# Modulation steps of the first MLP, two at every second place instead of one at each

## The chip, the cores and the metric

The kernel runs on one core of one Trainium2 chip, so there is one span and one granted clock to look at. The metric is the device time of one execution in microseconds (us): the median of several executions of the same program. A profile of one more execution gives the trace; times in it count from the start of its span.

## What is computed

A two-layer backbone for 128 context and 512 latent tokens of width 1024 (640 columns in all): layer 0 has attention and a convolution module, layer 1 a recurrent block, and each layer ends in an MLP. Every layer is modulated: six vectors of width 1024 for each of the two condition vectors come from one product with a large weight matrix.

```python
def _adaln(cond, w_mod, b_mod):
    return jnp.split(jax.nn.silu(cond) @ w_mod + b_mod, 6, axis=-1)

def _modulate(x, g, shift, scale):
    return _rmsnorm(x, g) * (1 + scale) + shift

def _sq_relu_mlp(h, w1, w2):
    return jnp.square(jax.nn.relu(h @ w1)) @ w2

# in each layer li, with ms = _adaln(cond_lat, w_mod[li], b_mod[li]) (mp likewise for the context):
y_s = y_s + ms[2] * os_
y_s = y_s + ms[5] * _sq_relu_mlp(_modulate(y_s, norm_ffn[li], ms[3], ms[4]), w_ff1[li], w_ff2[li])
```

## The kernel before

Activations lie transposed: 128 channels on the partitions, 640 token columns as two halves of 320. Products in full precision are made of three matmuls: weights and activations are split into a high part (`whi`, `hh`, `fh`; by a copy on ACT) and a low part (`wlo`, `hl`, `fl`; by a subtraction on DVE), and high x high, high x low and low x high are added up in PSUM (`product`, line 115, and `times`, line 809; every matmul is issued at line 113).

**An MLP** (`mlp`, line 724) goes over four groups `g` of 1024 hidden channels. In the up stage eight units `f` of 128 hidden channels each take 48 matmuls (`up`, line 756) into a PSUM tile `p2`, of which there are two; `hidden` (line 766) then normalizes the unit on DVE (`normed`, line 266: the product `fr`, then the small copy `bs`, after which the PSUM tile is free), applies relu and square on ACT, and at every second unit splits the pair of units into seven combinations for the down stage (`hidden_pair`, line 734). The down stage (`down`, line 806) is a fast 2x2 product: for each of four pairs `j` of output tiles seven blocks of 12 matmuls, some into the pair's `p2` tile, some into an extra bank `bu`. The last two blocks of a pair, `third_` and `fourth`, are put into the list `late` and issued within the next pair. The first unit of group `g+1` is made before the down stage of group `g`, the second one between its last two blocks.

**The modulation product** of the second layer is hidden in the MLP of the first. `mod_gen` (line 308) is a generator; one call of `next` is one **step**: it takes a buffer `mraw` (there are `NM` = 2), issues the transfer of 512 KB of `w_mod` from SyncE's queue (SP, line 313), and issues four matmuls of 32 stationary columns and 256 moving columns (`mod_mm`, line 289, matmul at line 292). The profile has eight records for the four matmuls of one step. Eight steps make one half of a `[128, 512]` PSUM tile, after which DVE transposes it (`mod_finish`, line 295). Three generators of 16 steps, 48 steps in all, stand in the list `fill` when the first MLP begins (line 909), and `filler(n)` (line 321) makes the next `n` steps, or fewer if none are left.

`filler(nfill)` is called at 56 **places** of an MLP: after each of the 32 units (line 772), and 24 times in the down stages, after `third_` and after `fourth` of the pair before (lines 837 and 845). In the first MLP `nfill` is 1, in the second 0. So the 48 steps lie one at each of the first 48 places: 14 places a group, the last one after unit 5 of group 3.

What is issued when on an engine is set by the framework's scheduler from the order of the program; weight transfers and splits have a priority of 4000 instructions ahead (`weights`, line 96, and `block`, line 789). Each engine, SP among them, then works off its own list in order.

Of the kernel before, what the change touches and what calls it, by code (L numbers as in the profile page):

```python
# [36 lines left out]
def backbone(ctx, tc, vecs, xT, wmod, w_att, w_ao, w_ff1, w_ff2, w_li, w_lo, w_lg, kcT, vc,  # L37
# [16 lines left out]
    def P2():  # L54
        if spare and next(turn_) % 3 == 2:
            return spare[0].tile([128, 2, 512], F32, name="p3", tag="p3")
        return ps.tile([128, 2, 512], F32, name="p2", tag="p2", bufs=2)
# [54 lines left out]
    def mm(o, w, v, start=False, stop=False, **kw):  # L112
        nc.tensor.matmul(o, w, v, start=start, stop=stop, **kw)  # L113
# [24 lines left out]
    def add_half(n, h, src, gate):  # L138
        for q, a, b, o, s in PIECE:
            if q == h:  # L140
                v = x[:, n, o:o + b - a]
                nc.vector.scalar_tensor_tensor(v, src[:, a:b], gate[:, n, s:s + 1], v, op0=ALU.mult, op1=ALU.add)  # L142
# [178 lines left out]
    def filler(n):  # L321
        while n and fill:
            try:
                next(fill[0])
                n -= 1
            except StopIteration:
                fill.pop(0)
# [396 lines left out]
    def mlp(l, pre, gate, pool, nfill, nxt, banks):  # L724
# [4 lines left out]
        def relu(r, p):  # L729
            bs = normed(r, p)  # L730
            for q, (a, b) in enumerate(SEG):
                nc.scalar.activation(r[:, a:b], r[:, a:b], AF.Relu, bias=bs[:, q:q + 1])  # L732

        def hidden_pair(r0, r1, all_):

            for r in (r0, r1):
                nc.scalar.activation(r, r, AF.Square)
            n = 8 if all_ else 7
            fh, fl = (pool.tile([128, n, 320], F32R, name=t, tag=t, bufs=4) for t in ("fh", "fl"))
            T = pool.tile([128, 4, 320], F32, name="T", tag="T")  # L740
            b12, b11, b22, b21 = r0[:, 0:320], r0[:, 320:640], r1[:, 0:320], r1[:, 320:640]
            nc.vector.tensor_tensor(T[:, 0], b12, b11, op=ALU.subtract)
            nc.vector.scalar_tensor_tensor(T[:, 1], b22, -1.0, T[:, 0], op0=ALU.mult, op1=ALU.subtract)
            nc.vector.tensor_tensor(T[:, 2], T[:, 1], b21, op=ALU.add)
            nc.vector.scalar_tensor_tensor(T[:, 3], b22, -1.0, b12, op0=ALU.mult, op1=ALU.subtract)
            for s, v in ((slice(0, 1), b11), (slice(1, 3), r1), (slice(3, 5), T[:, 0:2]), (slice(5, 7), T[:, 2:4]),
                         (slice(7, 8), b12))[:n - 3]:
                h, o = (t[:, s].rearrange("p k t -> p (k t)") for t in (fh, fl))
                if len(v.shape) > 2:
                    v = v.rearrange("p k t -> p (k t)")  # L750
                split(h, o, v)
            return fh, fl

        hid, held = {}, {}

        def up(g, f):
            wh, wl = weights(w_ff1[l, g * 8 + f])
# [8 lines left out]
        def hidden(g, f, p):  # L766
            r = held[f % 2] = pool.tile([128, 640], F32, name="fr", tag="t", bufs=4)
            pre.then(lambda: relu(r, p))
            if f % 2:
                r0 = held[0]  # L770
                pre.then(lambda: hid.update({f // 2: hidden_pair(r0, r, l == 1 and g == 3)}))
            filler(nfill)

        def both(g, f):
            hidden(g, f, up(g, f))

        def blocks_of(g, pairs):

            raw, k, t = {}, count(), []

            def ready(v):
                i = next(k) % 2
                if i == 0:
                    t[:] = parts_tile()
                o = slice(i * 512, i * 512 + 512)
                split(t[0][:, o], t[1][:, o], v)
                return t[0][:, o], t[1][:, o]

            def block(j, name):
                with tc.high_priority(offset=4000):  # L790
                    if name == "A11":
                        raw[j] = [raw_unit(w_ff2[l, g * 8 + 2 * j + i]) for i in range(2)]
                    X, Y = raw[j]
                    x0, x1, y0, y1 = X[:, 0:512], X[:, 512:1024], Y[:, 0:512], Y[:, 512:1024]
                    if name == "S1":
                        nc.vector.tensor_tensor(x0, x0, y0, op=ALU.subtract)
                        nc.vector.tensor_tensor(y0, y0, y1, op=ALU.subtract)
                    if name == "S2":
                        nc.vector.scalar_tensor_tensor(y0, x0, -1.0, y1, op0=ALU.mult, op1=ALU.subtract)
                    if name == "S4":  # L800
                        nc.vector.tensor_tensor(x1, x1, y0, op=ALU.add)
                    return ready(dict(A11=x0, A12=x1, A22=y1, S1=y0, S2=y0, S3=x0, S4=x1)[name])

            return block

        def down(g, pairs, between, done):
            block = blocks_of(g, pairs)

            def times(o, j, w, c, ks=range(4), start=True, wb=None):
                wh, wl = wb or block(j, w)  # L810
                for i in ks:
                    fh, fl = hid[i]
                    cs = slice(i * 128, i * 128 + 128)
                    vh, vl = fh[:, COMBO[c]], fl[:, COMBO[c]]
                    mm(o, wh[:, cs], vh, start=start and i == 0, skip_group_check=True)
                    mm(o, wh[:, cs], vl, skip_group_check=True)
                    mm(o, wl[:, cs], vh, stop=i == 3, skip_group_check=True)
                return wh, wl

            late = []  # L820

            def pair(j):
                p, u = P2(), U_[j % 2][:, 0:320]
                a, f = p[:, 0, 0:320], p[:, 1, 0:320]
                n0, n1 = 2 * j, 2 * j + 1
                if j == 0:
                    w1, w5 = times(a, j, "A11", "11", range(3)), times(f, j, "S1", "T1", range(3))
                    times(a, j, "", "11", [3], wb=w1)
                    times(f, j, "", "T1", [3], wb=w5)
                else:  # L830
                    times(a, j, "A11", "11")
                    times(f, j, "S1", "T1")
                nc.scalar.activation(u, a, AF.Copy)  # L833
                add_half(n1, 0, f, gate)
                while late:
                    late.pop(0)()
                    filler(nfill)
                    break
                times(a, j, "A12", "21", start=False)
                add_half(n0, 1, a, gate)  # L840
                times(u, j, "S2", "T2", start=False)
                add_half(n0, 0, u, gate)
                while late:
                    late.pop(0)()
                    filler(nfill)
                times(f, j, "S4", "22", start=False)
                add_half(n0, 0, f, gate)
                done(n0)

                def third_():  # L850
                    times(u, j, "S3", "T3", start=False)
                    add_half(n1, 0, u, gate)

                def fourth():
                    times(u, j, "A22", "T4", start=False)
                    add_half(n1, 1, u, gate)
                    done(n1)

                late.extend((third_, fourth))

            for j in pairs:
                pair(j)
            late.pop(0)()
            between()
            late.pop(0)()
# [3 lines left out]
        for g in range(4):  # L869
# [10 lines left out]
            def between(g=g):  # L880
                if g < 3:
                    begun[g + 1, 1] = up(g + 1, 1)
# [22 lines left out]
    with ExitStack() as ff:  # L905
        pool = ff.enter_context(tc.tile_pool(name="ff0", bufs=1, reuse_waits="tile"))
        banks = ff.enter_context(tc.tile_pool(name="pb0", bufs=1, space=PSUM, reuse_waits="tile"))
        for g in range(3):
            fill.append(mod_gen(1, g, mp))
        nm = mlp(0, nm, MOD[0, 2][:, 8:16], pool, 1,  # L910
                 lambda: Norm(pool, SC[1, 0], MOD[1, 0][:, 0:8]), banks)
# [171 lines left out]
    with ExitStack() as ff:  # L1083
        pool = ff.enter_context(tc.tile_pool(name="ff1", bufs=1, reuse_waits="tile"))
        banks = ff.enter_context(tc.tile_pool(name="pb1", bufs=1, space=PSUM, reuse_waits="tile"))
        mlp(1, nm, MOD[1, 2][:, 8:16], pool, 0, lambda: Final(pool), banks)
# [102 lines left out]
```

## Time and profile before

| | us |
|---|---|
| median of 3 runs | 1448.15 (1445.07 to 1448.96) |
| the profiled execution, its own time | 1448.06 |
| its span in the trace | 1446.3 |
| PE busy | 1403.6 (97% of the span) |
| weight loads (PEld) busy | 1307.6 (90%) |
| DVE busy | 1040.3 (72%) |
| ACT busy | 732.2 (51%) |

The 48 steps of the first MLP lie between 318.8 and 709 us of the span; the second MLP takes its last third. A group of matmul records shows its start, and a busy time that overlaps the next record, since matmuls are pipelined; the pace is read from start to start.

### The profile page before, as it was taken

What the parts mean: (1) busy time and instruction counts of PE and PEld (TensorE: products, weight loads), DVE (VectorE), ACT (ScalarE), POOL (GpSimd) and SP (SyncE); (2) the same over time, 40 slices, a digit from 0 to 9 for tenths busy, and PEclk for the clock granted to TensorE, in tenths of its full rate; (3) what the DMA queues carried; (4) which work ended last, traced back from release to release, by engine and by line L of the source; (5) the groups of instructions that cost most, each with busy time, mean ns of one, the idle gap of its engine ahead of it and who ended that gap; (6) DMA issues with size and microseconds to landing.
All of it is one profiled execution on the core that took longest, in us unless ns stands there. A gap on an engine that the chain in (4) does not pass through costs nothing.

```text
span 1446.3 us, 23687 instructions
## 1 busy us (share of the span) xinstructions
PE 1403.6 (97%) x9567; PEld 1307.6 (90%) x9567; DVE 1040.3 (72%) x1881; ACT 732.2 (51%) x1170; POOL 80.9 (6%) x122
## 2 busy tenths in 40 slices
PE   6999998999999999999999999999999999999998
PEld 4998563999999999999989999999999999999997
DVE  6699784675765675675588699997676676686673
ACT  5333377455434533533555878835643543544553
POOL 0000660000000000000000023100000000000000
PEclk9999899999999999999999999999999999999999
DMA  8523506224253244334212122122213113113112
GB/s 325 195 77 129 175 2 207 84 100 137 85 185 136 94 141 169 109 132 163 71 59 103 59 73 74 59 75 87 74 48 119 67 59 117 59 59 117 44 59 73
DMA packets 42909, 151.87 MB, mean 105 GB/s; under 512 B 4913, under 2 KB 5681, under 8 KB 42801
## 3 DMA queue, kind: packets, MB, share of 16 engines
q1 hardware_dynamic: 42800, 150.38, 29.8%
q8 instruction: 75, 1.23, 0.3%
q14 instruction: 34, 0.27, 0.1%
HBM read 147.60 MB, written 2.76 MB: 104 GB/s over the span
## 4 chain that ended last, share of the span: by engine, by line
PE 84%; DVE 7%; ACT 4%; DMA 2%; issue 1%; POOL 1%; SPq 0%; ACTq 0%; POOLq 0%
PE p L113 66%; PE bu L113 11%; PE p L292 4%; DMA mraw<-in_wmod 2%; DVE wlo L66 1%; PE p L428 1%; PE p L608 1%; DVE xc L968 1%; DVE ib L1027 1%; ACT whi L98 1%; PE p L604 1%; ACT hh L186 1%; DVE t L1019 0%; POOL dg L425 0%; DVE ib L1020 0%
## 5 line engine op out<-in xcount | busy, mean ns | idle before, releaser
L98 ACT ACTIVATE whi<-wraw 128x512 fp32r<-128x512 f32 (+1 forms) x327 | 246.3, 779 | 455.8 <-PE p L113 336.4
L113 PE MATMUL p<-hh,whi 128*128 128x320 f32 (+1 forms) x1512 | 462.6, 313 | 3.1 <-ACT hh L186 1.7
L113 PE MATMUL p<-hl,whi 128*128 128x320 f32 (+1 forms) x1512 | 460.1, 311 | 0.2 <-DVE hl L187 0.2
L113 PE MATMUL p<-hh,wlo 128*128 128x320 f32 (+1 forms) x1512 | 350.4, 310 | 0.0
L66 DVE TENSOR_TENSOR wlo<-wraw,whi 128x512 fp32r<-128x512 f32 (+1 forms) x327 | 280.0, 879 | 46.2 <-ACT whi L98 44.7
L113 PEld LDWEIGHTS p<-hh,whi 128*128 128x128 f32 x1512 | 285.9, 189 | 15.9 <-issue 7.8
L113 PEld LDWEIGHTS p<-hl,whi 128*128 128x128 f32 x1512 | 286.4, 189 | 0.9 <-DVE hl L187 0.8
L113 PEld LDWEIGHTS p<-hh,wlo 128*128 128x128 f32 x1512 | 256.8, 189 | 0.9 <-issue 0.8
L113 PE MATMUL p<-fh,whi 128*128 128x320 f32 x528 | 166.6, 316 | 4.0 <-ACT whi L98 1.1
L113 PE MATMUL p<-fl,whi 128*128 128x320 f32 x528 | 163.5, 310 | 2.0 <-DVE fl L66 2.0
L113 PE MATMUL p<-fh,wlo 128*128 128x320 f32 x528 | 163.3, 310 | 0.9 <-DVE wlo L66 0.9
L142 DVE SCALAR_TENSOR_TENSOR x<-p,mod,x 128x320 f32<-128x320 f32 (+2 forms) x228 | 96.5, 451 | 58.6 <-PE p L113 55.7
L268 DVE TENSOR_TENSOR fr<-p,R 128x640 f32<-128x640 f32 x64 | 52.7, 823 | 101.6 <-PE p L113 101.6
L113 PE MATMUL bu<-fh,whi 128*128 128x320 f32 x360 | 113.2, 314 | 0.3 <-ACT bu L833 0.3
L113 PEld LDWEIGHTS p<-fh,whi 128*128 128x128 f32 x528 | 99.5, 189 | 14.0 <-issue 5.1
L113 PE MATMUL bu<-fl,whi 128*128 128x320 f32 x360 | 112.2, 312 | 0.0
L113 PE MATMUL bu<-fh,wlo 128*128 128x320 f32 x360 | 112.0, 311 | 0.0
L732 ACT ACTIVATE fr<-fr,bs 128x512 f32<-128x512 f32 (+1 forms) x128 | 65.2, 555 | 78.6 <-DVE bs L270 78.4
L113 PEld LDWEIGHTS p<-fl,whi 128*128 128x128 f32 x528 | 99.5, 189 | 2.4 <-DVE fl L66 2.4
L113 PEld LDWEIGHTS p<-fh,wlo 128*128 128x128 f32 x528 | 99.3, 188 | 1.7 <-DVE wlo L66 1.7
L292 PE MATMUL p<-mraw,base 128*32 128x256 f32 x768 | 66.6, 419 | 15.2 <-DMA mraw<-in_wmod 15.0
L409 DVE SCALAR_TENSOR_TENSOR z<-u,vt,z 128x655 f32<-128x655 f32 x90 | 79.6, 911 | 0.4
(225 smaller groups left out, 2043.2 us busy)
## 6 DMA issues: line engine op xcount, KB each, us to landing
wraw<-in_w_ff SPq DMA_DIRECT2D x128, 512.0 KB, 3.5
mraw<-in_wmod SPq DMA_DIRECT2D x96, 512.0 KB, 3.9
wraw<-in_w_li SPq DMA_DIRECT2D x16, 512.0 KB, 3.4
wraw<-in_w_att SPq DMA_DIRECT2D x14, 512.0 KB, 3.6
wraw<-in_w_ao SPq DMA_DIRECT2D x8, 512.0 KB, 3.5
wraw<-in_w_lo SPq DMA_DIRECT2D x8, 512.0 KB, 3.5
x<-in_xT SPq DMA_DIRECT2D x4, 640.0 KB, 8.7
wraw<-in_w_lg SPq DMA_DIRECT2D x4, 512.0 KB, 3.4
```

Source lines behind the costliest of these rows:

```text
L66: nc.vector.tensor_tensor(out, full, f32(hi), op=ALU.subtract)
L98: nc.scalar.activation(hi, raw, AF.Copy)
L113: nc.tensor.matmul(o, w, v, start=start, stop=stop, **kw)
L142: nc.vector.scalar_tensor_tensor(v, src[:, a:b], gate[:, n, s:s + 1], v, op0=ALU.mult, op1=ALU.add)
L186: nc.scalar.activation(h, v, AF.Copy, scale=S[:, kt, s:s + 1])
L268: nc.vector.tensor_tensor(hy(o), p[:, :, 0:320], R, op=ALU.mult)
L292: nc.tensor.matmul(p[32 * q:32 * q + 32, half * 256:half * 256 + 256], base[:, kt], raw[:, q * 256:q * 256 + 256], start=(kt == 0), stop=( ...
L409: nc.vector.scalar_tensor_tensor(z, u[:, k:k + 655], wv[:, k:k + 1], z, op0=ALU.mult, op1=ALU.add)
L428: nc.tensor.matmul(p[:, 0:328], dg[:, d], u[:, o + k:o + k + 328], start=(k + i == 0), stop=(k == 30 and i == 2))
L604: nc.tensor.transpose(pt[:, b.kv, g * 128:g * 128 + 128], b.S[g][:, j * 128:j * 128 + 128], ident)
L608: nc.tensor.matmul(pav[c], vv[:, sl, c], th[:, b.kv], start=(j == 0), stop=(j == len(vs) - 1))
L732: nc.scalar.activation(r[:, a:b], r[:, a:b], AF.Relu, bias=bs[:, q:q + 1])
```

## The change

The calls of `filler` in the MLP go through a counter: at every second place nothing is done, at the others two steps are made one after the other. In the second MLP `2 * nfill` is still 0.

```diff
-        hid, held = {}, {}
+        hid, held, turns = {}, {}, count()
+
+        def two():
+
+            if next(turns) % 2:
+                filler(2 * nfill)
+
...
             if f % 2:
                 r0 = held[0]
                 pre.then(lambda: hid.update({f // 2: hidden_pair(r0, r, l == 1 and g == 3)}))
-            filler(nfill)
+            two()
...
                 add_half(n1, 0, f, gate)
                 while late:
                     late.pop(0)()
-                    filler(nfill)
+                    two()
                     break
...
                 while late:
                     late.pop(0)()
-                    filler(nfill)
+                    two()
```

How the instructions move is shown at three places. The names are those of the program with the number of the buffer. The first is PE in the up stage of group 0, at the ends of units 2 and 3. Before, at the end of unit 2 (`p_3199` is its tile, `p_3266` that of unit 3):

```order
L113 MATMUL p_3199<-hh,wlo 128x320
L113 MATMUL p_3199<-hh,wlo 128x322
L292 MATMUL p_3102<-mraw,base 32x256 x4
L113 MATMUL p_3266<-hh,whi 128x320
L113 MATMUL p_3266<-hl,whi 128x320
```

Now, at the end of unit 5 (`p_3411`), with nothing at the end of unit 4:

```order
L113 MATMUL p_3411<-hh,wlo 128x320
L113 MATMUL p_3411<-hh,wlo 128x322
L292 MATMUL p_3180<-mraw,base 32x256 x8
L113 MATMUL p_3501<-hh,whi 128x320
L113 MATMUL p_3501<-hl,whi 128x320
```

Rows of four modulation matmuls became half as many rows of eight. In the up stage these stand after units 1, 3, 5 and 7; in the down stage after `third_` of pairs 0, 1 and 2. The last two steps are made after unit 5 of group 3, as before.

The second is DVE at the top of the down stage of group 0. Before (`p_3657` is the tile of the first unit of group 1, whose release the down stage's second pair waits for):

```order
L66 TENSOR_TENSOR fl<-T,fh 128x640 x2
L66 TENSOR_TENSOR wlo<-wraw,whi 128x512 x2
L268 TENSOR_TENSOR fr<-p_3657,R 128x640
L796 TENSOR_TENSOR wraw<-wraw 128x512
L270 COPY bs<-p_3657 128x2
```

Now:

```order
L66 TENSOR_TENSOR fl<-T,fh 128x640 x2
L268 TENSOR_TENSOR fr<-p_3657,R 128x640
L66 TENSOR_TENSOR wlo<-wraw,whi 128x512 x2
L270 COPY bs<-p_3657 128x2
L802 TENSOR_TENSOR wraw<-wraw 128x512
```

`fr` went ahead of the two weight splits, and `bs`, which frees the tile, ahead of the combination of the next weights. On ACT, at the same place, the square of that unit went ahead of two weight splits and of the copy to `bu`.

The third is SP's queue over the down stage of group 0; `mraw` is one step's transfer, `wraw` one weight unit. Before:

```order
L313 DMA mraw<-in_wmod 128x1024 x3
L91 DMA wraw<-in_w_ff 128x1024 x2
L313 DMA mraw<-in_wmod 128x1024
L91 DMA wraw<-in_w_ff 128x1024
L313 DMA mraw<-in_wmod 128x1024
```

Now:

```order
L313 DMA mraw<-in_wmod 128x1024 x3
L91 DMA wraw<-in_w_ff 128x1024 x2
L313 DMA mraw<-in_wmod 128x1024 x2
L91 DMA wraw<-in_w_ff 128x1024 x2
L313 DMA mraw<-in_wmod 128x1024 x2
```

The two transfers of one place are now issued one behind the other, and the two weight units of a pair stand behind both.

## Rows read from the trace of the kernel before

**Rows 1.** The page: busy times, and the chain that ended last.

```profile
PE 1403.6 (97%) x9567; PEld 1307.6 (90%) x9567; DVE 1040.3 (72%) x1881; ACT 732.2 (51%) x1170; POOL 80.9 (6%) x122
...
PE 84%; DVE 7%; ACT 4%; DMA 2%; issue 1%; POOL 1%; SPq 0%; ACTq 0%; POOLq 0%
```

**Rows 2.** Windows of up stages, first and second MLP: busy per engine, PE clock, DMA.

```profile
443.80:498.90 55.10, 55.10 (x393) 50.88 (x393) 34.51 (x61) 29.58 (x47) 0.00 (x0) 1.00 0.36 125
1107.60:1158.00 50.40, 50.40 (x342) 50.40 (x341) 30.82 (x52) 25.95 (x39) 0.00 (x0) 1.00 0.22 74
```

**Rows 3.** The tile `mraw`, first MLP: instructions, ns min/median/max, first and last start.

```profile
L292 PE MATMUL p<-mraw,base x384: 379/391/403, 318.8 to 708.8; 128*32 128x256 f32 x192
```

**Rows 4.** Timeline, PE, one step between two units: start, us, instruction, count.

```profile
489.87 0.45 PE L113 MATMUL p<-hh,wlo 128*128 128x320 f32 x2
...
490.25 0.64 PE L292 MATMUL p<-mraw,base 128*32 128x256 f32 x8
...
491.08 0.31 PE L113 MATMUL p<-hl,whi 128*128 128x320 f32 x1
```

**Rows 5.** Timeline, PE, four steps in a row before the attention.

```profile
32.54 0.31 PE L113 MATMUL p<-hh,wlo 128*128 128x320 f32 x1
32.78 1.93 PE L292 MATMUL p<-mraw,base 128*32 128x256 f32 x32
...
34.89 0.31 PE L113 MATMUL p<-hh,whi 128*128 128x320 f32 x1
```

**Rows 6.** Timeline, PE, two steps in a row in the attention.

```profile
133.13 1.07 PE L292 MATMUL p<-mraw,base 128*32 128x256 f32 x16
```

**Rows 7.** The chain in order of time: a place that comes once a group, each MLP.

```profile
390.77 3.53 PE p L113 x24
...
507.78 3.53 PE p L113 x24
...
1068.95 3.23 PE p L113 x22
...
1175.78 3.23 PE p L113 x22
```

**Rows 8.** Timeline, PE, top of the second MLP's first down stage.

```profile
1062.53 0.31 PE L113 MATMUL p<-fh,wlo 128*128 128x320 f32 x1
1063.06 0.39 PE L113 MATMUL p<-fh,whi 128*128 128x320 f32 x1 [0.22 <-DVE bs L270]
```

**Rows 9.** Timeline, DVE, the same top of the down stage.

```profile
1060.22 1.29 DVE L66 TENSOR_TENSOR wlo<-wraw,whi 128x512 fp32r<-128x512 f32 x2
...
1062.15 0.68 DVE L796 TENSOR_TENSOR wraw<-wraw 128x512 f32<-128x512 f32 x1
1062.75 0.16 DVE L270 COPY bs<-p 128x2 f32<-128x2 f32 x1
```

**Rows 10.** Timeline, ACT and PE, top of a down stage of the first MLP.

```profile
503.45 0.42 ACT L833 ACTIVATE bu<-p 128x320 f32<-128x320 f32 x1
503.80 0.72 ACT L737 ACTIVATE fr<-fr 128x640 f32<-128x640 f32 x1
...
504.10 0.31 PE L113 MATMUL bu<-fh,whi 128*128 128x320 f32 x1
```

**Rows 11.** The page, DMA issues: KB each, median us to landing.

```profile
wraw<-in_w_ff SPq DMA_DIRECT2D x128, 512.0 KB, 3.5
mraw<-in_wmod SPq DMA_DIRECT2D x96, 512.0 KB, 3.9
```

**Rows 12.** Timeline, SP, down stage of group 1 in the first MLP.

```profile
513.70 0.33 SPq L313 DMA_DIRECT2D mraw<-in_wmod  x1
518.71 0.33 SPq L91 DMA_DIRECT2D wraw<-in_w_ff  x1
...
523.60 0.33 SPq L91 DMA_DIRECT2D wraw<-in_w_ff  x1
```

**Rows 13.** Timeline, DVE, there: the first use of those weights.

```profile
527.46 0.68 DVE L796 TENSOR_TENSOR wraw<-wraw 128x512 f32<-128x512 f32 x1
```

## The prediction

> **What bounds the kernel.** I read the page first, then the busy time by stage, then single places in the timeline. On the page PE is busy for 97% of the span and makes 84% of the chain that ended last [rows 1]. In a window of the first MLP's up stage PE is busy for all of its 55.10 us at a granted clock of 1.00, which is the 2.4 GHz level, while DVE takes 34.51 and ACT 29.58 us of it [rows 2]. So in this stage PE alone sets the end: whatever PE no longer does there shortens the run by as much, as long as DVE, ACT and the transfers keep up. The window of the second MLP gives the undisturbed pace, since no modulation lies in it: 342 matmuls in 50.40 us, 0.1474 us from start to start [rows 2].
>
> The steps that the change regroups are 384 matmul records in the first MLP, eight a step, 48 steps [rows 3].
>
> **What one step costs now.** The last two matmuls of a unit are issued at 489.87 and one pace later; then comes the step at 490.25; the second matmul of the next unit starts at 491.08 [rows 4]. From 489.87 to 491.08 are three intervals between matmuls of the units, which would take 3 x 0.147 = 0.44 us; they take 1.21. A lone step costs 0.77 us of PE time, in which the eight records themselves span 0.64.
>
> The windows say the same without this one place: 55.10 us hold seven units and seven steps (393 records), so 337 matmuls of the units at 0.1474 us, 49.66 us, leave 5.44 us, 0.78 us a step [rows 2].
>
> **What two steps in a row would cost.** The trace has no pair inside an MLP, but it has steps in a row elsewhere at the same clock. Four in a row stand between matmuls of the same kind: from 32.54 to 34.89 there are two intervals, 0.29 us by the pace, and 2.35 us pass, so four steps cost 2.06 us [rows 5]. Three more steps therefore cost 2.06 - 0.77 = 1.29 us, 0.43 each. Two in a row show 1.07 us of records against 0.64 for one, again 0.43 more [rows 4, 6]. So a visit to the modulation matmuls costs 0.34 us once and 0.43 us for each step made in it. A pair costs 1.20 us where two lone steps cost 1.54.
>
> A rule speaks against this. The Trainium skill, TensorEngine Tiling, Instruction Overhead, gives each matmul an overhead of about 60 cycles; by it the overhead goes with the number of matmuls, a pair costs twice a lone step and the sum is nought. The trace does not agree: three further steps in one visit cost 0.43 each where the first costs 0.77 [rows 4, 5]. That the price goes by matmuls is kept as a rival.
>
> **The sum.** 24 visits disappear: 24 x 0.34 = 8.1 us less on PE, all of it on the path. The number of matmuls, transfers, weight splits and evacuations is unchanged, and the 24 pairs end at the same place as the 48 steps did, after unit 5 of group 3, so the wait at group 3's down stage, which no step covers now either, stays.
>
> **What lone steps covered.** The second MLP runs the same groups without steps. One group takes 507.78 to 390.77 = 117.01 us in the first MLP and 1175.78 to 1068.95 = 106.83 in the second, 10.18 apart [rows 7]. Fourteen lone steps are 14 x 0.77 = 10.78. So a group without steps has 0.6 us of waits that the steps now hide. One is at the top of the down stage: PE should have gone on at 1062.68 and starts at 1063.06, when `bs` has freed the tile [rows 8]; ahead of `bs` on DVE stand two weight splits and a combination of weights [rows 9]. In the changed kernel no step stands between the early unit and the down stage any more, but a pair of 1.20 us stands ahead of that unit, which lets DVE finish the last pair of units by so much earlier; and `bs` is now issued ahead of the combination, 0.6 us earlier. Against a delay of 0.38 us that is enough, so I take nothing for this wait.
>
> On ACT the square, 0.72 us, now stands ahead of the copy that `bu` needs [rows 10]. Before, that copy was done at 503.87, 0.2 us ahead of the first matmul on `bu` [rows 10]; by the new order I find it level with it or up to 0.2 us late. I take 0.1 us a group, 0.3 in all. The bounds: nothing at the low end; at the high end all of the covered waits and a whole square in each of three groups, 3 x (0.6 + 0.72) = 4.0 us.
>
> **Transfers.** A pair needs both `mraw` buffers filled. They come free when the pair before is done, at least 12 us earlier (one pair of output tiles, seven blocks of 12 matmuls at 0.147; two units take 14), and a transfer lands 3.9 us after its issue, 7.8 us for two if they take turns [rows 11]. I cost this at nothing; the cover is over 4 us.
>
> So the profiled execution, 1448.06 us in its own time, less 8.1 and plus 0.3, gives 1440.3 us; the median of the runs shown is 0.1 above that execution, so **1440.4 us**, 0.5% faster.
>
> **Rivals.** *The covered waits come back whole.* For it: the second MLP shows them [rows 7, 8]. Against it: a pair stands before the early unit. Price 3 x 0.6 = 1.8 us instead of 0.3: 1441.9 us.
>
> *The price hangs on the number of matmuls.* Then a pair costs 1.54 us and the time stays at 1448.1. For it: nothing in the rows; against it the four in a row and the two in a row, which agree on 0.43 [rows 5, 6]. They ran before the MLP, though, with other work beside them. If the scheduler had pulled the two steps of a pair apart, the time would be the same; the rows of eight on PE's list exclude that.
>
> *Slower: weight units wait behind pairs of transfers.* SP works in order, and now two modulation transfers stand directly ahead of a down pair's two weight units. The second weight unit of pair 3 is issued at 523.60 [rows 12], needs 3.5 us [rows 11], and is used at 527.46 [rows 13]: 0.36 us to spare. If it were held back by one transfer's 3.9 us, DVE and then PE would lose 3.5 us. Two such pairs in each of three groups make 6 x 3.5 = 21 us, less the 7.8 gained: 1461 us. It decides from a delay of 1.7 us each (7.8 / 6 = 1.3 lost, beside 0.36 spare). Against it: the modulation transfers are released with the visit and issued at 513.70 [rows 12], 5 us before the first of these weight units and 10 us before the second, which wait for DVE and not for the queue; two transfers of 3.9 us are over by then.
>
> **How the numbers follow.** A measurement of this kernel can tell about 0.3%, 4.3 us, from no change. Chances: forecast 0.82, covered waits whole 0.08, price by number 0.06, slower 0.04. The first two are faster by 7.8 and 6.3 us; of their 0.90 I move 0.04 to "within", because the runs before spread over 3.9 us. So faster 0.86, within 0.3% 0.10, slower 0.04. The high end of the range is the whole give-back, 1448.1 - 8.1 + 4.0 = 1444.0 us. The low end is no give-back, 1440.1, less the 3.1 us by which the fastest run lay under the median: 1437.0.
>
> **What would show it.** In the profile after: 24 groups of 16 modulation records in the first MLP, each spanning about 1.07 us; 117.01 - 7 x 0.34 = 114.6 us from group to group there, and 106.8 as before in the second MLP; no wait of PE for `mraw`. Groups of 117 us would mean that the price goes by matmuls; idle time of PE that `bs` or the copy to `bu` ends at the top of a down stage, that cover is lost; idle time that `wlo` ends late in a down stage, that weights come late.

## Result, and the profile after

The changed kernel takes **1437.82 us** (median of 6 runs, 1435.7 to 1440.6); the kernel before, beside it, 1448.56 us (6 runs). The ratio is 0.9926, with a 95% interval of 0.991 to 0.9943: 10.7 us less, where 7.8 were forecast. The profiled execution took 1435.7 us by its own time, with a span of 1433.9. In a later comparison one execution of the kernel before took 2805.6 us; it is left out of every figure here.

The page after, busy times, the chain, and the two kinds of transfer:

```profile
PE 1388.9 (97%) x9567; PEld 1303.9 (91%) x9567; DVE 1039.6 (73%) x1881; ACT 731.7 (51%) x1170; POOL 80.5 (6%) x122
PE 84%; DVE 7%; ACT 4%; DMA 3%; issue 1%; POOL 1%; SPq 0%; ACTq 0%; POOLq 0%; DVEq 0%
wraw<-in_w_ff SPq DMA_DIRECT2D x128, 512.0 KB, 3.5
mraw<-in_wmod SPq DMA_DIRECT2D x96, 512.0 KB, 4.4
```

Against [rows 1], PE has lost 14.7 us of busy time and DVE and ACT under 1; the bound is the same. A modulation transfer takes 0.5 us longer to land than in [rows 11]; of those issued between 330 and 700 us the median rose from 3.5 to 4.8, which fits the two of a place being under way together.

One pair between two units, from PE's timeline of the changed kernel:

```profile
484.30 0.45 PE L113 MATMUL p<-hh,wlo 128*128 128x320 f32 x2
484.68 1.07 PE L292 MATMUL p<-mraw,base 128*32 128x256 f32 x16
485.69 0.42 PE L113 MATMUL p<-hh,whi 128*128 128x320 f32 x1
485.94 0.31 PE L113 MATMUL p<-hl,whi 128*128 128x320 f32 x1
```

Read as [rows 4] were: from 484.30 to 485.94 pass 1.64 us, three intervals of 0.147 would be 0.44, so the pair costs 1.20 us. All 24 pairs cost 1.19 to 1.20, 28.7 us in all; the 48 lone steps of before cost 0.76 to 0.77, 36.7 in all. The difference is 8.0 us.

The chain in order of time, at the place of [rows 7], the three of the first MLP and the first two of the second:

```profile
387.63 3.24 PE p L113 x22
...
502.23 3.23 PE p L113 x22
...
616.88 3.24 PE p L113 x22
...
1056.73 3.23 PE p L113 x22
...
1163.56 3.23 PE p L113 x22
```

A group of the first MLP takes 114.60 and 114.65 us now, against 117.01 before; one of the second takes 106.83, as before. The windows of two down stages, group 1 of the first MLP and the first of the second (columns as in [rows 2]):

```profile
492.89:551.25 58.36, 58.36 (x422) 55.96 (x421) 39.12 (x73) 19.03 (x34) 0.00 (x0) 1.00 0.42 145
1046.94:1102.30 55.36, 55.13 (x374) 54.64 (x373) 39.64 (x73) 19.14 (x34) 0.00 (x0) 1.00 0.28 96
```

In the first, where modulation is made, PE has no idle time. With three pairs taken off (3 x 1.20), the first is 54.8 us long, 0.6 shorter than the second without any.

**Where the 12.4 us between the two spans lie.** I took the start of the same two matmuls in each trace: the first one of unit 1 of group 0 in the first MLP, and the 2424th from there (counting those of line 113), which is in group 3's up stage behind the last step.

| us | to the first matmul | first MLP, 2423 matmuls on | from there to the last matmul |
|---|---|---|---|
| before | 317.72 | 394.89 | 728.50 |
| after | 316.47 | 386.57 | 725.69 |

Two thirds, 8.32 us, lie in the stretch that the change touches. The other 4.1 lie outside. Part of them stands out in the windows right behind the waits of group 3's down stage, of before and of after:

```profile
732.90:736.30 3.40, 3.40 (x15) 3.40 (x14) 0.96 (x2) 0.00 (x0) 0.00 (x0) 0.50 0.42 154
```

```profile
722.90:726.30 3.40, 3.40 (x24) 3.40 (x24) 1.39 (x3) 0.00 (x0) 0.00 (x0) 1.00 0.43 154
```

The same matmuls run there at a granted clock of 0.50, the 1.2 GHz level, in the one execution (15 in 3.40 us) and of 1.00, the 2.4 GHz level, in the other (24). Ahead of both stretches PE waited at the same four matmuls for as long. The execution of before has seven stretches at 0.50, 39.5 us together, that of after four, 22.2 us.

In all ten traces with 32 stationary columns, those of the experiments below included, the time behind the stretch goes by how long the clock is at 0.50 there, and not by the change. With 15 to 17 us at that level it takes 725.7 to 726.5 us (the kernel before with three buffers, 726.1, among them), with 18 to 19 it takes 726.7 to 727.4, and with 22 it takes 728.3 to 728.5 (pairs at the other places, 728.3, among them).

### The profile page after: what moved, and what is told of

Same layout as the page of the kernel before. It is cut to its first block, busy times and chain, and to the rows that moved or that the text cites. A ratio compares the mean times of both kernels' runs of the same rounds, so it can differ in the third digit from the quotient of the medians.

```text
span 1433.9 us, 23690 instructions
## 1 busy us (share of the span) xinstructions
PE 1388.9 (97%) x9567; PEld 1303.9 (91%) x9567; DVE 1039.6 (73%) x1881; ACT 731.7 (51%) x1170; POOL 80.5 (6%) x122
## 4 chain that ended last, share of the span: by engine, by line
PE 84%; DVE 7%; ACT 4%; DMA 3%; issue 1%; POOL 1%; SPq 0%; ACTq 0%; POOLq 0%; DVEq 0%
PE p L113 66%; PE bu L113 11%; DMA mraw<-in_wmod 3%; PE p L292 3%; DVE wlo L66 1%; PE p L608 1%; PE p L428 1%; DVE xc L974 1%; DVE ib L1033 1%; PE p L604 1%; ACT whi L98 1%; DVE t L1025 0%; POOL dg L425 0%; DVE ib L1026 0%; PE p L259 0%
## 5 line engine op out<-in xcount | busy, mean ns | idle before, releaser
L292 PE MATMUL p<-mraw,base 128*32 128x256 f32 x768 | 61.3, 413 | 17.7 <-DMA mraw<-in_wmod 12.6
```

Source lines behind the costliest of these rows:

```text
L292: nc.tensor.matmul(p[32 * q:32 * q + 32, half * 256:half * 256 + 256], base[:, kt], raw[:, q * 256:q * 256 + 256], start=(kt == 0), stop=( ...
```

## The experiments

### Both kernels again

No edit. Is the rest beyond 8 us the change's, or a matter of the executions drawn?

> The kernel before, unchanged, for the granted clock of each of its executions. The trace of the change saves 8.3 us inside the first MLP (24 visits at 0.344) and 4 us more at places that the change does not touch, where the trace of before ran at the lower clock level and the trace of the change did not. Theory: how often the clock falls differs from execution to execution and not with the kernel. Then these executions spread over several us as those of the change do (1435.7 to 1440.6), the longer ones at the lower mean clock (0.985 to 0.993 as there), and a profile of this kernel with another set of falls than the one shown. Rival: the kernel before falls to the lower level each time after the wait at group 3's down stage (733 us in its trace), the changed one does not; then every execution here has a mean clock of 0.987 or less and the fall at 733 us stands in this profile again.

> The changed kernel, unchanged. Theory: 8.3 us under the kernel before at the same mean clock, 1440 plus or minus 2 us, clocks of 0.985 to 0.993, and in its profile a fall of the clock at other places than in the first profile, possibly after group 3's wait too. Rival: over 10 us under the kernel before again, clocks of 0.990 and more, no fall after group 3's wait.

The kernel before as a candidate came out at 1446.41 us (12 runs), ratio 0.9988 (0.9973 to 1.0002); the changed one at 1439.84 us (6 runs), ratio 0.9936 (0.9914 to 0.9958). The profiled execution of the changed kernel was 8.1 us longer than the first one, with nine stretches at half clock, 56.3 us together, and still 386.64 us for the stretch of the first MLP. The second profile of the kernel before fell to half clock at the same five places behind the first MLP as the first one, group 3's waits among them (733.9 us), as the rival had it; but its executions ran at mean clocks of 0.986 to 0.993, and the changed kernel now fell at these waits too (728.8). The kernel before ran 37 times in this comparison and in that of the runs with three buffers, the changed one 12 times in the first comparison and this: the means are 1447.6 and 1438.7 (standard deviations 2.4 and 2.5), 8.9 us apart, give or take 1.6. At like mean granted clock they are 8.3 apart at 0.988 (6 and 5 runs) and 10.0 at 0.990 (3 and 2 runs). So the first measurement's 10.7 fits a change of 8 to 9 us, and executions that happened to fall well for the rest.

### Threes instead of pairs

```diff
-    NM = 2
+    NM = 3
-            if next(turns) % 2:
-                filler(2 * nfill)
+            if next(turns) % 3 == 2:
+                filler(3 * nfill)
```

> Three steps at every third place with three buffers: 16 visits instead of 24. Theory (a visit costs 0.34 us, a step 0.43): 16 x 1.63 = 26.1 us of modulation against 24 x 1.20 = 28.7, so 2.7 us under the change. In group 1 no step stands between unit 6 and the down stage, so there PE should wait 0.4 to 0.5 us for the early unit's tile, as the second MLP does; 2.2 us under the change in all. Rival (the price goes by the number of matmuls, and the change gained elsewhere): the time of the change, plus the 0.5 us.

It took 1429.69 us (6 runs, 1428.78 to 1435.02), ratio 0.9875 (0.9853 to 0.9898), further down than threes alone should bring. But the stretch of the first MLP took 386.29 us, 0.3 less than with pairs, where 2.2 were expected: the gain does not lie there. Two things had been left out. The third buffer helps ahead of the first MLP, which began 7.6 us earlier in this execution (more on that below). And the scheduler pulled steps apart: 20 visits stand in the trace and not 16, and they cost 28.2 us together, not 26.1. One of them is a single matmul, two records:

```profile
487.98 0.31 PE L113 MATMUL p<-fh,wlo 128*128 128x320 f32 x1
488.21 0.62 PE L292 MATMUL p<-mraw,base 128*32 128x256 f32 x2
...
489.01 0.31 PE L113 MATMUL p<-fl,whi 128*128 128x320 f32 x1
```

From 487.98 to 489.01 are 1.03 us; two intervals would take 0.29. This one matmul costs 0.74 us, almost what a whole step of four costs (0.77), and the visit of eleven that follows costs 1.62, like those of twelve. A visit of five matmuls costs 1.18, nearly what eight cost. So the price goes neither by the matmul nor by the record: the four column tiles of a step run side by side (their records start 0.007 us apart), and a visit has its own price.

The single matmul stands at the top of group 1's down stage, where the wait for `bs` was expected. No wait shows there, though `bs` was done only at 488.33, after this matmul had begun:

```profile
488.18 0.15 DVE L270 COPY bs<-p 128x2 f32<-128x2 f32 x1
```

### The same product on the whole array, in pairs and in lone steps

The first run is the changed kernel with this edit (wide pairs), the second the kernel before with it (wide lone steps). All four matmuls of a step then add into the same 128 rows, so neither computes the right modulation:

```diff
-    base = mp.tile([128, 8, 32], F32, name="base")
+    base = mp.tile([128, 8, 128], F32, name="base")
-            nc.tensor.matmul(p[32 * q:32 * q + 32, half * 256:half * 256 + 256], base[:, kt],
-                             raw[:, q * 256:q * 256 + 256], start=(kt == 0), stop=(kt == 7))
+            nc.tensor.matmul(p[:, half * 256:half * 256 + 256], base[:, kt],
+                             raw[:, q * 256:q * 256 + 256], start=(kt == 0 and q == 0), stop=(kt == 7 and q == 3))
```

> The change, with all 128 stationary columns in the modulation matmuls (the 32 that hold data and 96 of zeros), so that the four matmuls of a step run one after the other over the whole array instead of side by side on a quarter each; all four add up in the same columns of PSUM, so the modulation values are not those of the reference. The fp32 matmul on ones in the MLP's norm already shows an fp32 visit over the whole array without any fixed cost (four records of 0.267 us between matmuls of the units, 1.36 us for two intervals of 0.147 and 1.07 of records). Theory (the fixed 0.34 us belongs to the change between the whole array and its quarters): a step costs 16 passes of 0.107 = 1.7 us, a pair 3.4 us, the four in a row 6.8 us, with nothing left over: a pair is half of the four in a row. Rival (it belongs to the change of data type or to leaving the units' matmuls at all): a pair 3.75 us, the four in a row 7.15 us. The whole: about 24 x 2.2 = 53 us longer than the change by the theory, 61 by the rival, plus what the steps ahead of the MLP take more.

> The kernel before with the same replacement in its modulation products as the wide run: 128 stationary columns, the four matmuls of a step adding into the same 128 rows, so the modulation it computes is another one. Lone steps at 48 places against the wide run's 24 pairs. There a pair takes the place of 3.45 us, which is eight matmuls of 0.427 and 0.04 over. Theory: the 0.34 us of a visit belong to 32 column tiles among matmuls on the whole array, so wide steps have no price per visit: a lone step costs half a pair, 1.72 us, and the time inside the first MLP is that of the wide pairs within 1 us (48 x 1.72 = 82.6 against 24 x 3.45 = 82.8). Rival: any change of the operand type or of the stationary matrix's source costs 0.34 a visit and was hidden in the pairs' figure; then a lone wide step costs 1.9 to 2.1 us and the first MLP is 8 us longer than with wide pairs.

They took 1536.88 and 1534.36 us (one execution each). PE's timeline, a wide pair:

```profile
517.53 0.46 PE L113 MATMUL p<-hh,wlo 128*128 128x320 f32 x2
517.83 3.62 PE L292 MATMUL p<-mraw,base 128*128 128x256 f32 x16
...
521.43 0.31 PE L113 MATMUL p<-hl,whi 128*128 128x320 f32 x1
```

and a wide lone step:

```profile
517.61 0.46 PE L113 MATMUL p<-hh,wlo 128*128 128x320 f32 x2
517.91 1.89 PE L292 MATMUL p<-mraw,base 128*128 128x256 f32 x8
...
519.78 0.31 PE L113 MATMUL p<-hl,whi 128*128 128x320 f32 x1
```

The pair takes the place of 3.90 - 0.44 = 3.46 us, the lone step of 2.17 - 0.44 = 1.73: exactly half. The stretch of the first MLP takes 440.61 us with 24 wide pairs and 440.97 with 48 wide lone steps. With 32 stationary columns the same regrouping is worth 8.3 us, with 128 nothing that shows. Ahead of the attention, where the scheduler had pulled the four steps in a row apart, one wide matmul alone takes the place of 0.43 us, and fourteen in a row take that of 6.05, fourteen times as much. So a change of the operands' type, of the moving data's source or of the PSUM bank between a unit and a step costs nothing here; the 0.34 us of a visit go with the 32-column tiles. (The edit changes the number of stationary columns and the tiling together; the two are not told apart.)

Where the price lies can be seen in the weight loads (PEld), for the pair of the changed kernel shown above and for the wide pair:

```profile
484.16 0.33 PEld L113 LDWEIGHTS p<-hh,wlo 128*128 128x128 f32 x2
484.68 0.59 PEld L292 LDWEIGHTS p<-mraw,base 128*32 128x32 f32 x16 [0.19 <-issue]
485.68 0.19 PEld L113 LDWEIGHTS p<-hh,whi 128*128 128x128 f32 x1 [0.41 <-ACT whi L98]
```

```profile
517.39 0.33 PEld L113 LDWEIGHTS p<-hh,wlo 128*128 128x128 f32 x2
517.68 3.36 PEld L292 LDWEIGHTS p<-mraw,base 128*128 128x128 f32 x16
521.07 0.19 PEld L113 LDWEIGHTS p<-hh,whi 128*128 128x128 f32 x1
```

Between units and wide steps the loads follow one another without a gap. Around column tiles they stop for 0.19 to 0.20 us on the way there and 0.41 on the way back, the same at all 48 lone steps of before and all 24 pairs, so the 0.41 are hardly a wait for `whi`, as the profile puts it. The Trainium skill, TensorEngine Tiling (Array Packing), Key Properties, says that changing the tiling mode drains the engine, without a figure. The runs agree with it: the gaps are there with column tiles and not without, and 0.34 us is what going there and back costs.

### Three buffers, with pairs and with lone steps

The first run is the changed kernel, the second the kernel before, both with

```diff
-    NM = 2
+    NM = 3
```

> The change with three buffers for the transfers of a step (NM = 3) instead of two; the pairs stay at every second place. The run with threes was 7.6 us ahead of the changed kernel before the first MLP began and lost 1.1 us of that within it. Theory: the 7.6 us belong to the third buffer (steps ahead of the first MLP wait less for transfers), so this run has them too, keeps the 24 pairs at 1.20 us each and 114.6 us a group, and comes out 7.6 us under the changed kernel: about 1431 us, a ratio of 0.988 to the kernel before. Rival: the 7.6 us were an accident of that execution's granted clock; then this run lies within 2 us of the changed kernel, 1437 to 1441 us.

> The kernel before with three buffers (NM = 3): lone steps at each of 48 places. Against the run with three buffers and pairs it differs by the change alone, from another start. Theory: the change is worth 24 x 0.34 = 8.1 us less 0.2 at the copy to the extra bank, so this run is 8 us above the other, groups take 117.0 us against 114.6, and lone steps cost 0.77. Rival: what the first measurement showed beyond that (10.7 us) belongs to the change as well, in places outside the first MLP; then it is 10 to 11 us above. Rival by buffers: with a third buffer a lone step is cheaper, since no transfer ends late; then under 7 us.

With pairs: 1433.44 us (5 runs, 1427.53 to 1433.73), ratio 0.9887 (0.987 to 0.9905). With lone steps: 1438.79 us (5 runs, 1436.69 to 1440.39), ratio 0.9936 (0.9923 to 0.995). In the chain, the place of [rows 7] with pairs,

```profile
383.99 3.24 PE p L113 x22
...
498.59 3.25 PE p L113 x22
```

and with lone steps:

```profile
381.83 3.53 PE p L113 x24
...
498.83 3.53 PE p L113 x24
```

114.60 and 117.00 us a group, as with two buffers, and 386.60 against 394.83 us for the whole stretch: the change is worth 8.2 us from this start too. The buffer does not touch the price of a visit. The medians are only 5.4 apart, less than the 8 that were expected; the means are 1431.8 and 1438.9, 7.1 apart. The two profiled executions are 3.2 us apart (spans of 1431.7 and 1434.9), and there it can be seen why: the one with lone steps began the first MLP 4.0 us earlier (308.79 against 312.83) though the programs are the same up to there, with 6.8 us at half clock around 138 us against 13.7, and the one with pairs fell to half clock again behind group 3's waits. That the granted clock accounts for the medians too is likely, but five runs each don't show it. With pairs the third buffer was to bring 7.6 us and 1431; the first MLP began 3.6 us earlier than in the first profile after (312.83 against 316.47), and the median is 4.4 under that kernel's. Over the ten traces with 32 stationary columns, unit 1 of the first MLP begins at 308.8 to 312.8 us with three buffers (5 traces) and at 316.5 to 323.3 with two (5 traces). So the third buffer helps; by how much differs from execution to execution.

Part of what the third buffer does ahead of the MLP is plain in PE's waits there. The changed kernel, 208.03 to 252.18 us, waits by line and in total, times, longest:

```profile
PE p L292 <- DMA mraw<-in_wmod: 4.9, 5, 1.9
```

With three buffers, the same matmuls, 208.68 to 248.52:

```profile
PE p L292 <- DMA mraw<-in_wmod: 1.9, 2, 1.4
```

The stretch is 44.15 us long with two buffers and 39.84 with three: 4.3 us less, 3.0 of them in these waits.

### Pairs at the other places

```diff
-            if next(turns) % 2:
+            if next(turns) % 2 == 0:
```

> The change with the pairs at the other places: after units 0, 2, 4 and 6 and directly ahead of the down stage instead of ahead of the early unit. It asks what hides the wait for the small copy that frees the tile. Theory: a visit costs the same wherever it stands, and a pair directly ahead of the down stage hides that wait at least as well; 24 pairs at 1.20 us, 114.6 us a group within 0.2, no gap of 0.07 us at the copy to the extra bank in those groups, time within 3 us of the changed kernel. Rival: only a pair ahead of the early unit lets DVE come early enough; then 0.4 to 0.6 us of waiting appears once a group at the top of the down stage and a group takes 115.0 to 115.2 us.

One execution took 1438.87 us, 1.0 over the changed kernel's median. The chain at the place of [rows 7]:

```profile
388.75 3.53 PE p L113 x24
...
503.46 3.52 PE p L113 x24
...
618.18 3.53 PE p L113 x24
```

Groups of 114.71 and 114.72 us; the stretch of the first MLP takes 386.93, 0.36 more. The delay at the copy to `bu` is gone, and a new one of 0.08 to 0.09 us stands once a group between the extra bank and the next pair's tile. A pair ahead of the early unit and a pair behind it hide the wait for `bs` alike.

### The same pairs, all in the first half

```diff
-    NM = 2
+    NM = 3
-            filler(nfill)
+            filler(2 * nfill)
```

On the kernel before, and so at its other two calls.

> Three buffers, and two steps at each of the first 24 places instead of at every second one: the same 24 pairs, but none from group 1's first down pairs on. It asks what the pairs near the top of a down stage hide. Theory: a pair costs 1.20 us here too; group 2, which now has no step, shows the waits of the second MLP: 106.8 us from group to group, 0.6 us more than 114.6 - 7 x 1.20 = 106.2, with PE waiting some 0.4 us at the top of the down stage for the copy that frees the tile. In all about 0.6 us more inside the first MLP than with the pairs spread out. Rival: nothing was hidden by the pairs; then group 2 takes 106.2 us. Second rival: two transfers a place (every 8.5 us) keep the queue so busy that weights or steps come late; then PE waits for a buffer mraw or for wlo in groups 0 and 1, and visits cost more than 1.20.

One execution took 1431.94 us. The down stage of group 2, which has no step, by its window, and the top of it in PE's timeline:

```profile
609.73:665.10 55.37, 55.14 (x375) 54.65 (x373) 39.56 (x73) 19.19 (x34) 0.00 (x0) 1.00 0.28 96
```

```profile
613.11 0.31 PE L113 MATMUL p<-fh,wlo 128*128 128x320 f32 x1
613.65 0.39 PE L113 MATMUL p<-fh,whi 128*128 128x320 f32 x1 [0.23 <-DVE bs L270]
```

The wait of [rows 8] is back at the top: 0.54 us from start to start, 0.39 too many, and the stage is as long as in the second MLP. From the end of group 2's second unit to that of group 3's pass 106.8 us. So the 0.6 us which the prediction subtracted from a group are real, they lie in the down stage, and the pairs do hide them. No visit cost more than 1.20, and PE waited neither for `mraw` nor for `wlo`: two transfers every 6.5 to 8.3 us were no burden. The stretch took 387.99 us, 1.4 more than with spread pairs, not 0.6: groups 0 and 1 lost some 0.4 each as well, 0.2 to 0.3 of it in the down stage, though a pair stood ahead of the early unit in both. What of this is which delay was not followed further.

### The last pair inside group 3's waits

On the kernel with three buffers and pairs:

```diff
-            if next(turns) % 2:
+            if next(turns) % 2 and next(visits) < 23:
...
                     w1, w5 = times(a, j, "A11", "11", range(3)), times(f, j, "S1", "T1", range(3))
+                    if g == 3:
+                        filler(2 * nfill)
                     times(a, j, "", "11", [3], wb=w1)
```

> The run with three buffers and pairs, with the last pair taken from the end of unit 5 of group 3 and made in the middle of group 3's first down pair, where PE waits for DVE some 3.4 us in all. Theory: there a pair of 1.20 us lies in idle time of PE, so the time falls by 1.2 us against the run with three buffers and pairs, and the gaps there shrink by as much. Rival: PE works in order, and the pair lies ahead of matmuls that are ready before the long wait, or the long wait lies ahead of the pair, so that nothing of it is covered: the time stays. If the granted clock no longer falls to half behind the wait, up to 1.5 us more are gained.

1429.18 us (4 runs, 1425.47 to 1430.17), ratio 0.9861 (0.9843 to 0.9879). PE's timeline at these waits in the changed kernel:

```profile
719.41 0.41 PE L113 MATMUL p<-fh,whi 128*128 128x320 f32 x1 [0.57 <-ACT fh L98]
...
720.82 0.42 PE L113 MATMUL p<-fl,whi 128*128 128x320 f32 x1 [0.99 <-DVE fl L66]
...
721.95 0.41 PE L113 MATMUL p<-fh,whi 128*128 128x320 f32 x1 [0.57 <-ACT whi L98]
...
722.68 0.42 PE L113 MATMUL p<-fh,wlo 128*128 128x320 f32 x1 [0.16 <-DVE wlo L66]
```

and with the pair in them:

```profile
710.05 1.07 PE L292 MATMUL p<-mraw,base 128*32 128x256 f32 x16
...
714.34 0.42 PE L113 MATMUL p<-fl,whi 128*128 128x320 f32 x1 [0.66 <-DVE fl L66]
...
715.48 0.41 PE L113 MATMUL p<-fh,whi 128*128 128x320 f32 x1 [0.57 <-ACT whi L98]
...
716.21 0.41 PE L113 MATMUL p<-fh,wlo 128*128 128x320 f32 x1 [0.17 <-DVE wlo L66]
```

The wait for `fh` is gone and the one for `fl` is a third shorter: idle time of 2.29 us became 1.40, and the gaps from start to start shrank by 1.2, the whole price of the pair. The path from the last unit through DVE, which sets the end of these waits, is as long as before. This execution kept the 2.4 GHz level behind the waits; the lone steps with three buffers and the first profile after did so with all four waits in place, so the cover is not shown to be the reason. Of the 4.3 us between the medians of this run and of pairs with three buffers, 1.2 are shown. Its median is the lowest of the study, but the threes are only 0.5 above it, and the two intervals overlap.

## Why the prediction was right, point by point

- **PE alone bounds the stage**: right. In the first MLP the time removed from PE is the time gained, and there is no wait of PE for `mraw` in it.
- **A visit costs 0.34 us, a step 0.43**: right; a pair was to cost 1.20 and cost 1.20. The price, read from four steps in a row ahead of the attention and two within it, held between units of an MLP, in 24 groups of 16 records of 1.07 us. Groups came out at 114.60 where 114.6 stood in the forecast; that this fits so closely is in part luck, for two small terms offset each other (see the size).
- **The rival by number of matmuls**: fell. The number is the same, the gain is there, and one matmul alone costs 0.74 us. The Trainium skill, TensorEngine Tiling (Array Packing), Instruction Overhead, speaks of some 60 cycles each; the traces do not agree that the price of a visit goes by it.
- **0.1 us a group given back at the copy to `bu`**: right in place, a little high in size. ACT and PE there:

```profile
497.96 0.42 ACT L839 ACTIVATE bu<-p 128x320 f32<-128x320 f32 x1
```

```profile
498.47 0.38 PE L113 MATMUL bu<-fh,whi 128*128 128x320 f32 x1
498.68 0.31 PE L113 MATMUL bu<-fl,whi 128*128 128x320 f32 x1
```

  The copy was done at 503.87 for a matmul at 504.10 before [rows 10]; now it is done at 498.38 for one at 498.47. The next start is 0.21 us later instead of 0.147: 0.07 lost, once a group.
- **Covered waits stay covered**: right, and the pair-free group shows that there was something to cover.
- **Transfers cost nothing**: right; a pair's two transfers and the weight units behind them on SP's queue,

```profile
507.85 0.80 SPq L313 DMA_DIRECT2D mraw<-in_wmod  x2
513.75 3.96 SPq L91 DMA_DIRECT2D wraw<-in_w_ff  x2
```

  stand 5.9 us apart; with a median of 4.8 us to landing the modulation transfers are mostly over by then, as the case against the slower rival had it, and PE does not wait in the whole stretch.
- **The size**: 7.8 us forecast, 8.3 in the stretch of the first MLP, 8.9 ± 1.6 over all runs, 10.7 in the first comparison. The sum's terms were sized nearly right. The three intervals around the visits account for 8.0 us, and 0.2 and not 0.3 came back at the copy to `bu`, which leaves 7.8; the stretch shows 8.3. By the groups a visit counts (2.41 + 0.07) / 7 = 0.354 us rather than 0.34: some 0.02 us of its price lie in matmuls beyond the three intervals, as the 0.78 us a step of the windows in the prediction already had it against 0.77. What the sum had no term for is that one execution may hold twice as much time at half clock as another. The range allowed for it by the 3.1 us from median to fastest run. The median of 1437.82 lies 2.6 us under the forecast and 0.8 above the low end: the mechanism gave 8 to 9 us, and the rest was the draw of executions.

## What to carry to other kernels

Where small matmuls on column tiles are strewn among matmuls on the whole array, the trip there and back has a price of its own (0.34 us here) that no matmul's record shows; it is found from the starts of the matmuls on both sides of a stay of one, two and four steps, and from gaps between the weight loads. Put as many of them into one stay as buffers allow, leave some stay near each place where PE would wait, and look in the order of instructions whether the scheduler has kept them together. Before a difference between two traces is put down to a change, cut both at the same matmuls: what lies outside the stretch that was changed may be the clock's, as the granted clock there can show.

## What was not expected of the hardware

- The same waits of PE are followed by 3.4 us at 1.2 GHz in some executions and not in others. In such a stretch nine matmuls fewer are made (15 against 24), 1.3 us at the pace of 0.147; runs of one program spread over 9 us, the longer ones with a lower mean clock: before, 1443.1 us at 0.993 and 1452.3 at 0.984.
- One 32-column matmul alone costs nearly what four on neighbouring column tiles cost, 0.74 us against 0.77.
- A third buffer for the transfers, needed for the threes in the first MLP, paid ahead of it, 4.3 us in the window of the attention shown, and nothing in the MLP.
